# Weaving the blocks of w_down among those of w_up, with TensorE's order written out

## The chip, the cores and the metric

The kernel runs on one core of one Trainium2 chip. A core has TensorE (PE; its weight loads are listed apart as PEld), VectorE (DVE), ScalarE (ACT), GpSimd (POOL), a sync engine (SP) that issues plain loads and stores, and 16 DMA engines. The metric is the device time of one execution in microseconds, lower is better; the median of three runs is given.

## The reference

One decoder block on 512 tokens of width 1024, all in float32. Only the end of it bears on the change:

```python
merged = jax.nn.sigmoid(gate_a) * y_a + jax.nn.sigmoid(gate_b) * y_b
h = x + merged @ w_out[l]                     # 512x1024 @ 1024x1024
hn = rmsnorm(h, norm_mlp_g[l])
x = h + jnp.square(jax.nn.relu(hn @ w_up[l])) @ w_down[l]   # 1024 -> 4096 -> 1024
```

Ahead of it come a combined projection, a gated delta rule and a forgetting attention, which give y_a and y_b; with the gates they take the first 649 us, and the change touches them only where it is said below.

## The kernel before

**Precision.** Every float32 product is made of three float32r products: a matrix x is split into hi (x rounded to float32r, a cast on ScalarE) and lo (x minus hi, a subtraction on VectorE), and hi*hi + hi*lo + lo*hi are added up in PSUM. So each weight and each activation needs one cast and one subtraction before TensorE can use it.

**Seven products for eight.** w_o, w_up (w_u) and w_down (w_d) are cut in quarters, and a 2 x 2 block product is made of seven products P1 to P7 in Winograd's manner. w_up and w_down are worked through in four chunks c of 1024 of the 4096 hidden columns. So there are nine such block products: w_o, then for each chunk w_up and w_down. Each product has two units (`s_` 0 and 1), and a unit is one 128 x 1024 weight tile: 9 x 7 x 2 = 126 units. A unit of w_o or w_d is 12 matmuls of 512 columns, one of w_u 24 of 256.

*Weights* (`load`, L158): P1, P2 and P3 read a quarter fresh, on SP's queue; P5, P6, P4 and P7 add another quarter onto the tile of an earlier product (`FACTOR`, L144) by an accumulating DMA on GpSimd's queue, which must wait until VectorE has made the earlier product's low part. A ring of three raw tiles for each `s_` holds them. The look-ahead is `LA_RAW` = 3 and `LA_NEW` = 6 units for loads, `LA_SPLIT` = 2 for hi and lo (four buffers each; L203 casts, L204 subtracts).

*Activations* (`act_forms`, L927): P1, P2 and P4 take a quarter as it is, P5, P6, P3 and P7 a sum of quarters (L937 to L946), made on GpSimd for h and for the chunks, on VectorE for w_o. Then cast (L948) and low part (L949).

**Order.** `tokens_product` (L989) runs a whole block product of w_o or w_d in the order P1, P2, P5, P3, P6, P7, P4 and has VectorE add the PSUM banks into eight accumulator pages (L998). `mlp_up` (L1090) does the same for w_u, and evicts with a copy, or an addition, and relu and square on ScalarE (L1098 to L1110). One ends before the other is emitted: w_o, u0, d0, u1, d1, u2, d2, u3, d3. Between w_o and u0 lies the norm of h: squares on ScalarE (L1048), the inverse root (L1052 to L1054), scaling (L1061; the left half on VectorE, the right half on GpSimd), transposes on TensorE (L1067), and copies into the quarters `hq` (L1070). The blocks U, V and W of PSUM are chains of two banks; P1, P6, P7 and P4 go on in U, P5 and P3 in V.

What is emitted is not yet the order: a planner with a model of the engines orders each engine's instructions by priority (the place in the program) and readiness, gives out buffers from the free ones of a pool, and puts in the waits. The additions and evictions were given an earlier priority with `tc.high_priority(offset=AHEAD)`.

Of the kernel before, what the change touches and what calls it, by code (L numbers as in the profile page):

```python
# [16 lines left out]
P = 128  # L17
# [7 lines left out]
NACC = 12  # L25
NMM = 3
# [4 lines left out]
LA_NEW = 6  # L31
# [3 lines left out]
AHEAD = 150  # L35


def hybrid_block(tc, a, out):
# [24 lines left out]
    TAGS = {"junk": 2, "proj": 3}  # L63
# [83 lines left out]
    def product_units(w, c):  # L147
        return [(p, (w, c, s_)) for p in ORDER for s_ in range(NSUB)]

    seq += product_units("w_o", 0)  # L150
    for c in range(NC):
        seq += product_units("w_u", c) + product_units("w_d", c)
# [3 lines left out]
    fresh = [None, None]  # L156

    def load(n):  # L158
        nme, i = seq[n]
        if nme in FACTOR:  # L160
            w, c, s_ = i
            q, old = FACTOR[nme]
            if old is None:
                raw = fresh[s_].tile([P, D], F32, tag="raw", name=nm("draw"))
                nc.sync.dma_start(raw, a[w][c, q, s_])
            else:
                raw = factors[old, i]
                nc.gpsimd.dma_start(raw, a[w][c, q, s_], accum_op=ALU.add)
# [15 lines left out]
    def prefetch_new(n):  # L184

        for m in range(pos[0], min(len(seq), n)):
            if m not in raws and seq[m][0] in FACTOR and FACTOR[seq[m][0]][1] is None and fresh[0]:
                load(m)
# [725 lines left out]
    fresh[:] = [wraw, ctx.enter_context(tc.tile_pool(name="draw", bufs=3))]  # L914
# [12 lines left out]
    def act_forms(q, res, s_, order=("P1", "P2", "P5", "P6", "P3", "P7", "P4"), eng=None):  # L927


        eng = eng or vec  # L930
        for p in order:
# [3 lines left out]
            elif p == "P7":  # L935
                x = q[1, 0]
                eng.tensor_tensor(x, q[0, 0], x, op=ALU.subtract)  # L937
            elif p == "P5":
                x = s1 = accpage("s")
                eng.tensor_tensor(x, q[1, 0], q[1, 1], op=ALU.subtract)  # L940
            elif p == "P6":
                x = s2 = accpage("s")
                eng.tensor_tensor(x, s1, q[0, 0], op=ALU.subtract)
            else:
                x = accpage("s")
                eng.tensor_tensor(x, q[0, 1], s2, op=ALU.add)  # L946
            hi, lo = page(F32R, "shi"), page(F32R, "slo")
            act.copy(hi, x)  # L948
            vec.tensor_tensor(lo, x, hi[:, :].bitcast(F32), op=ALU.subtract)  # L949
            res[p, s_] = hi, lo  # L950
            yield

    def make(forms, gens, *products):
        for p in products:
            for s_ in range(NSUB):
                while (p, s_) not in forms:
                    next(gens[s_])
# [3 lines left out]
    mgens = [act_forms(merged[s_], mforms, s_) for s_ in range(NSUB)]  # L961
# [6 lines left out]
    for n in range(KT):  # L968
# [4 lines left out]
        for i in range(2):  # L973
            pool.tensor_tensor(of_half(merged[s_][i, j], f), of_half(sg, i), of_half(ma[n], i), op=ALU.add)
        for _ in range(2 if n >= 4 else 0):
            next(mgens[0], None)
# [12 lines left out]
    def tokens_product(w, c, gens, forms, done):  # L989


        chains, left = {}, {(0, 0): 2, (0, 1): 2, (1, 1): 2, (1, 0): 2 if w == "w_o" else 1}

        def add(i, l, ps, op):
            for t in range(2):
                acc = accs[2 * i + t][l]
                with tc.high_priority(offset=AHEAD):
                    vec.tensor_tensor(acc, acc, ps[t], op=op)  # L998
            left[i, l] -= 1
            if not left[i, l]:  # L1000
                done(i, l)

        for n, p in enumerate(ORDER):
            make(forms, gens, *ORDER[:n + 3])
            b, first = BANKS[p]
            if w == "w_o" and p == "P4":
                b, first = "X", True
            if first:
                chains[b] = [atps("down"), atps("down")]
            ps = chains[b]  # L1010
            for s_ in range(NSUB):
                whi, wlo = unit(p)
                shi, slo = forms[p, s_]
                for t in range(2):
                    for f in range(2):
                        wh, wl = whi[:, f * T:(f + 1) * T], wlo[:, f * T:(f + 1) * T]
                        k = slice(f * 256 + t * P, f * 256 + (t + 1) * P)
                        last = s_ == NSUB - 1 and f == 1
                        mm(ps[t], shi[:, k], wh, start=first and s_ == 0 and f == 0, stop=False, skip_group_check=True)  # L1019
                        mm(ps[t], slo[:, k], wh, start=False, stop=False, skip_group_check=True)  # L1020
                        mm(ps[t], shi[:, k], wl, start=False, stop=last, skip_group_check=True)  # L1021
                tick()
            if p in ("P1", "P2"):
                add(0, 0, ps, ALU.add)
            elif p == "P5":
                add(1, 1, ps, ALU.add)
            elif p == "P6":
                add(0, 1, ps, ALU.subtract)
            elif p == "P3":
                add(0, 1, ps, ALU.add)  # L1030
            elif p == "P7":
                if w == "w_o":
                    add(1, 0, ps, ALU.add)
                add(1, 1, ps, ALU.subtract)
            else:
                add(1, 0, ps, ALU.add)
# [4 lines left out]
    hgens = [act_forms(hq[s_], hforms, s_, eng=pool) for s_ in range(NSUB)]  # L1041
# [3 lines left out]
    def square_h(i, l):  # L1045
        for t in range(2):
            junk = page(s="junk")
            act.activation(junk, accs[2 * i + t][l], AF.Square, accum_out=ss_h[:, 2 * i + t, l:l + 1])  # L1048

    def normalise_h(i):  # L1050
        sl = slice(2 * i, 2 * i + 2)
        vec.tensor_tensor(rs_h[:, sl], ss_h[:, sl, 0], ss_h[:, sl, 1], op=ALU.add)  # L1052
        vec.tensor_scalar(rs_h[:, sl], rs_h[:, sl], 1.0 / D, EPS, op0=ALU.mult, op1=ALU.add)
        rsq(rs_h[:, sl], rs_h[:, sl])  # L1054
        for l in range(2):
            if i:
                yield
            hn = []
            for t in range(2):
                x = page(s="proj")  # L1060
                (pool if l else vec).tensor_scalar(x, accs[2 * i + t][l], rs_h[:, 2 * i + t:2 * i + t + 1], None, op0=ALU.mult)  # L1061
                hn.append(x)
            for j in range(2):
                pt = atps("hnT")
                for f in range(2):
                    for t in range(2):
                        nc.tensor.transpose(pt[:, f * 256 + t * P:f * 256 + (t + 1) * P], hn[t][:, cs(2 * j + f)], ident)  # L1067
                for f in range(2):
                    n = 4 * l + 2 * j + f
                    act.activation(of_half(hq[l][i, j], f), of_half(pt, f), AF.Copy, scale=mlp_g[:, n:n + 1])  # L1070
                if i == 0:
                    next(hgens[l])
        if i:
            make(hforms, hgens, "P5")
        yield
# [3 lines left out]
    def h_done(i, l):  # L1079
        square_h(i, l)  # L1080
        ready[i] -= 1
        if not ready[i]:
            ht.append(start(normalise_h(i)))
            if i == 0:
                finish(ht[0])

    ht = []
    tokens_product("w_o", 0, mgens, mforms, h_done)

    def mlp_up(c):  # L1090

        qs, chains, forms = quarters("act"), {}, {}
        gens = [act_forms(qs[s_], forms, s_, ("P1", "P2", "P4", "P5", "P6", "P3", "P7"), pool) for s_ in range(NSUB)]

        def evict(p, q, ps):

            if p == "P1":
                act.copy(q[0, 0], ps)  # L1098
            elif p == "P5":
                act.copy(q[1, 1], ps)  # L1100
            elif p == "P3":
                act.copy(q[0, 1], ps)
            elif p == "P4":
                act.activation(q[1, 0], ps, AF.Relu)
                act.activation(q[1, 0], q[1, 0], AF.Square)
            else:
                x, op = {"P2": (q[0, 0], ALU.add), "P6": (q[0, 1], ALU.subtract), "P7": (q[1, 1], ALU.subtract)}[p]
# [117 lines left out]
```

## Time and profile before

| | us |
|---|---|
| runs | 1056.85, 1056.90, 1054.27 (median 1056.85) |
| the profiled execution | 1054.39, its span 1052.7 |
| TensorE busy in the span | 1011.4 (96%) |
| VectorE, ScalarE, GpSimd busy | 688.7 (65%), 560.2 (53%), 285.1 (27%) |
| mean granted TensorE clock | 0.987 |
| DMA | 138.67 MB, mean 132 GB/s |

A matmul counts as busy up to its modelled end, which overlaps the next one, so TensorE's share says little about its pace; the starts of matmuls do. Low parts of weights (L204) carry 169.2 us of VectorE in this stage, of activations (L949) less. The time is to be read by stretches of the span, since the stages have different limits.

### The profile page before, as it was taken

How to read it: one execution, taken by the hardware profiler on the slowest of the kernel's cores; microseconds unless marked ns; L12 is line 12 of the kernel's file. 1: busy time of each engine (PE TensorE's matmuls, PEld its weight loads, DVE VectorE, ACT ScalarE, POOL GpSimd, SP SyncE). 2: the span in 40 equal slices, each digit the busy share in tenths (PEclk: the TensorE clock that was granted, in tenths of full speed). 3: DMA queues.
4: the chain of work that ended last, by engine and by line, in shares of the span. 5: the costliest groups of instructions: out<-in, count | busy, mean ns of one | idle time of the engine just before them, and what ended most of it. 6: DMA issues, size and time to landing. Idle time of an engine off the chain costs nothing.

```text
span 1052.7 us, 16282 instructions
## 1 busy us (share of the span) xinstructions
PE 1011.4 (96%) x6361; PEld 890.5 (85%) x6361; DVE 688.7 (65%) x1092; ACT 560.2 (53%) x855; POOL 285.1 (27%) x256
## 2 busy tenths in 40 slices
PE   9999999999999999999999999979899989989988
PEld 7788899998788999988888887779689869968966
DVE  6867777353678694445553238787885785686685
ACT  7674354355754545457633324485736735744751
POOL 1455120115343111021100034262421422251160
PEclk9999999999999999999999999999999999989999
DMA  6444323134233221325444336865589688777854
GB/s 216 142 127 138 92 85 95 60 101 140 71 120 109 72 91 52 92 100 148 133 160 160 100 109 155 197 140 137 124 176 199 156 168 186 182 144 174 189 114 116
DMA packets 58732, 138.67 MB, mean 132 GB/s; under 512 B 6208, under 2 KB 22816, under 8 KB 58656
## 3 DMA queue, kind: packets, MB, share of 16 engines
q1 hardware_dynamic: 48256, 99.88, 30.1%
q0 software_dynamic: 10400, 37.76, 20.7%
q8 instruction: 50, 0.82, 0.3%
q14 instruction: 26, 0.21, 0.1%
HBM read 129.18 MB, written 8.44 MB: 131 GB/s over the span
## 4 chain that ended last, share of the span: by engine, by line
PE 81%; DVE 10%; issue 4%; ACT 2%; DMA 1%; POOL 1%; SPq 0%; DVEq 0%; ACTq 0%; POOLq 0%
PE up L1130 14%; PE mm L222 9%; PE mm L223 9%; PE mm L226 9%; PE down L1021 4%; PE fx L810 4%; PE fx L813 4%; PE fx L811 4%; PE down L1019 4%; PE down L1020 4%; DVE lo L204 3%; DVE slo L949 2%; PE fo L793 2%; PE sc L768 2%; DVE acc L998 1%
## 5 line engine op out<-in xcount | busy, mean ns | idle before, releaser
L204 DVE TENSOR_TENSOR lo<-draw,hi 128x1024 fp32r<-128x1024 f32 x126 | 169.2, 1346 | 81.4 <-ACT hi L203 80.5
L203 ACT CAST hi<-draw 128x1024 fp32r<-128x1024 f32 x126 | 131.8, 1049 | 156.5 <-PE down L1020 76.9
L204 DVE TENSOR_TENSOR lo<-raw,hi 128x1024 fp32r<-128x1024 f32 (+1 forms) x90 | 111.8, 1248 | 87.6 <-PE mm L226 53.8
L203 ACT CAST hi<-raw 128x1024 fp32r<-128x1024 f32 (+1 forms) x90 | 91.9, 1029 | 110.4 <-PE mm L223 81.6
L222 PE MATMUL mm<-uhi,hi 128*128 128x512 f32 x344 | 136.1, 397 | 2.8 <-DVE conv L510 2.2
L223 PE MATMUL mm<-ulo,hi 128*128 128x512 f32 x344 | 136.6, 398 | 1.2 <-DVE ulo L237 1.2
L1021 PE MATMUL down<-lo,shi 128*128 128x512 f32 x280 | 111.4, 404 | 14.1 <-DVE lo L204 14.1
L1020 PE MATMUL down<-hi,slo 128*128 128x512 f32 x280 | 112.6, 403 | 6.4 <-DVE slo L949 6.4
L1019 PE MATMUL down<-hi,shi 128*128 128x512 f32 x280 | 109.8, 401 | 1.7 <-DVE sgb L972 0.9
L1130 PE MATMUL up<-slo,hi 128*128 128x256 f32 x448 | 92.6, 287 | 6.3 <-DVE slo L949 6.3
L810 PE MATMUL fx<-hi,uhi 128*128 128x256 f32 x384 | 97.9, 290 | 0.2 <-DVE conv L510 0.2
L811 PE MATMUL fx<-hi,ulo 128*128 128x256 f32 x384 | 96.0, 285 | 0.0
L1130 PE MATMUL up<-shi,hi 128*128 128x256 f32 x448 | 91.5, 285 | 1.7 <-ACT shi L948 1.1
L1130 PE MATMUL up<-shi,lo 128*128 128x256 f32 x448 | 90.3, 285 | 0.0
L226 PE MATMUL mm<-uhi,lo 128*128 128x512 f32 x344 | 89.2, 395 | 0.0
L222 PEld LDWEIGHTS mm<-uhi,hi 128*128 128x128 f32 x344 | 64.7, 188 | 17.7 <-issue 3.9
L223 PEld LDWEIGHTS mm<-ulo,hi 128*128 128x128 f32 x344 | 64.7, 188 | 15.4 <-DVE ulo L237 2.3
L1021 PEld LDWEIGHTS down<-lo,shi 128*128 128x128 f32 x280 | 54.7, 196 | 27.0 <-DVE lo L204 15.6
L1130 PEld LDWEIGHTS up<-slo,hi 128*128 128x128 f32 x448 | 71.0, 194 | 7.0 <-DVE slo L949 6.9
L226 PEld LDWEIGHTS mm<-uhi,lo 128*128 128x128 f32 x344 | 63.6, 188 | 13.3 <-issue 0.5
L810 PEld LDWEIGHTS fx<-hi,uhi 128*128 128x128 f32 x384 | 73.4, 191 | 1.2 <-issue 0.9
L811 PEld LDWEIGHTS fx<-hi,ulo 128*128 128x128 f32 x384 | 73.4, 191 | 0.5 <-issue 0.2
(309 smaller groups left out, 2112.7 us busy)
## 6 DMA issues: line engine op xcount, KB each, us to landing
draw<-w_u POOLq DMA_DIRECT2D x32, 512.0 KB, 6.9
draw<-w_d POOLq DMA_DIRECT2D x32, 512.0 KB, 5.6
raw<-w_gdn SPq DMA_DIRECT2D x24, 512.0 KB, 3.6
raw<-w_fox SPq DMA_DIRECT2D x24, 512.0 KB, 3.6
draw<-w_u SPq DMA_DIRECT2D x24, 512.0 KB, 4.2
draw<-w_d SPq DMA_DIRECT2D x24, 512.0 KB, 4.1
row<-rowd SPq DMA_DIRECT2D x24, 256.0 KB, 5.1
raw<-w_ga SPq DMA_DIRECT2D x8, 512.0 KB, 4.0
```

Of the source, the lines that this page charges most:

```text
L203: act.copy(hi[:, c], raw[:, c])
L204: vec.tensor_tensor(lo[:, c], raw[:, c], hi[:, c].bitcast(F32), op=ALU.subtract)
L222: mm(o, w, rhi(k), start=(k == 0), stop=False)
L223: mm(o, w, rlo(k), start=False, stop=False)
L226: mm(o, lo[:, k * cols:(k + 1) * cols], rhi(k), start=False, stop=(k == KT - 1))
L810: mm(o, uhi[k][:, cs(tb)], w, start=(k == 0), stop=False)
L811: mm(o, ulo[k][:, cs(tb)], w, start=False, stop=False)
L813: mm(o, uhi[k][:, cs(tb)], us[k // 4][1][:, (k % 4) * 256:(k % 4 + 1) * 256], start=False, stop=(k == KT - 1))
L1019: mm(ps[t], shi[:, k], wh, start=first and s_ == 0 and f == 0, stop=False, skip_group_check=True)
L1020: mm(ps[t], slo[:, k], wh, start=False, stop=False, skip_group_check=True)
L1021: mm(ps[t], shi[:, k], wl, start=False, stop=last, skip_group_check=True)
L1130: mm(o, wx[:, (2 * kb + f) * P:(2 * kb + f + 1) * P], of_half(hforms[p, j][part], kb % 2), start=first and f == 0 and part == 0 and wx is ...
```

## The change

- The 126 units get one written order, `MLP`. The units of w_d of a chunk stand among the last ones of w_u of the same chunk and the first ones of w_u of the next: for chunks after the first, w_u P5, w_d P4 of the chunk before, w_u P3, P6, P7, P4, w_d P1, P2, P5, w_u P1 of the next chunk, w_d P3, P6, w_u P2 of the next chunk, w_d P7. The last chunk has w_d P4 of the chunk before between its w_d P1 and P2, and its own P4 in banks of its own (as w_o).
- One loop over `MLP` takes the place of `tokens_product`'s and `mlp_up`'s loops. In each step it emits, in this order: transposes that are due, the cast of a weight, the evictions of the step before, the low part of the weight, loads, then small tasks on activations from a list `later`, up to two operations of VectorE in a step (three in w_o and in w_u's first chunk), and then the matmuls.
- TensorE's instructions of this part stay in program order (`tc.keep_in_program_order`). VectorE and ScalarE can be pinned in the same way from a given step on; with `PIN` = (400, 400, 0) and 126 steps they are not. The earlier priority of evictions goes.
- The sums of activations are made on VectorE, as is the whole scaling of h.
- P2's fresh tiles get a ring of their own with two tiles; the look-ahead is `LA_MLP` = 3 for hi and lo, `LA_RAW_MLP` = 5 and `LA_NEW` = 7 for loads; "proj" pages are four, not three. In the stage before, two half tasks (sum and cast, or low part) are taken after a product of w_pf where a whole one was taken twice.

```diff
     ORDER = ("P1", "P2", "P5", "P3", "P6", "P7", "P4")
+    MLP = [("w_o", 0, p, s_) for p, s_ in (("P1", 0), ("P2", 0), ("P1", 1), ("P2", 1))]
+    MLP += [(w, 0, p, s_) for w, ps in (("w_o", ORDER[2:]), ("w_u", ORDER[:2])) for p in ps for s_ in range(NSUB)]
+    for c in range(NC):
+        more = c + 1 < NC
+        MLP += [(w, c_, p, s_) for w, c_, p in (
+            ("w_u", c, "P5"), ("w_d", c - 1 if more else -1, "P4"), ("w_u", c, "P3"), ("w_u", c, "P6"), ("w_u", c, "P7"),
+            ("w_u", c, "P4"), ("w_d", c, "P1"), ("w_d", -1 if more else c - 1, "P4"), ("w_d", c, "P2"), ("w_d", c, "P5"),
+            ("w_u", c + 1, "P1"), ("w_d", c, "P3" if more else "P6"), ("w_d", c, "P6" if more else "P3"),
+            ("w_u", c + 1, "P2"), ("w_d", c, "P7")) for s_ in range(NSUB) if 0 <= c_ < NC]
+    MLP += [("w_d", NC - 1, "P4", s_) for s_ in range(NSUB)]
...
-                raw = fresh[s_].tile([P, D], F32, tag="raw", name=nm("draw"))
+                raw = fresh[2 if nme == "P2" else s_].tile([P, D], F32, tag="raw", name=nm("draw"))
...
+        def __getattr__(self, op):
+            f = getattr(self.eng, op)
+            return (lambda *args, **kw: tc.keep_in_program_order(f(*args, **kw))) if self.pinned[0] else f
...
+    def form_task(q, res, p, s_, steps):
+        if "a" in steps:
...
+                if p == "P5":
+                    pvec.tensor_tensor(x, q[1, 0], q[1, 1], op=ALU.subtract)
+                elif p == "P6":
+                    pvec.tensor_tensor(x, res["P5", s_, "x"], q[0, 0], op=ALU.subtract)
...
+        if "b" in steps:
+            hi = res[p, s_, "hi"]
+            lo = page(F32R, "slo")
+            pvec.tensor_tensor(lo, res[p, s_, "x"], hi[:, :].bitcast(F32), op=ALU.subtract)
...
-                with tc.high_priority(offset=AHEAD):
-                    vec.tensor_tensor(acc, acc, ps[t], op=op)
...
-                (pool if l else vec).tensor_scalar(x, accs[2 * i + t][l], rs_h[:, 2 * i + t:2 * i + t + 1], None, op0=ALU.mult)
+            pvec.tensor_scalar(x, accs[2 * i + t][l], rs_h[:, 2 * i + t:2 * i + t + 1], None, op0=ALU.mult)
...
+    for k, (w, c, p, s_) in enumerate(MLP):
+        for pin, first in zip(pins, PIN):
+            pin[0] = k >= first
+        used = 0
+        for f, *args in before:
+            f(*args)
+        del before[:]
+        n = pos[0]
+        pos[0] += 1
+        new = range(len(units), min(len(seq), n + 1 + LA_MLP))
+        for m in new:
+            hi, lo = whl.tile([P, D], F32R, tag="hi", name=nm("hi")), whl.tile([P, D], F32R, tag="lo", name=nm("lo"))
+            pact.copy(hi, raws[m][0])
+            units.append((hi, lo))
+        for f, *args in evicted:
+            f(*args)
+            used += f is add_task or (f is evict and args[0] in ("P2", "P6", "P7"))
+        for m in new:
+            hi, lo = units[m]
+            pvec.tensor_tensor(lo, raws[m][0], hi[:, :].bitcast(F32), op=ALU.subtract)
+        prefetch_raw(n + 1 + LA_RAW_MLP)
+        prefetch_new(n + 1 + LA_NEW)
+        res = {"w_o": mforms, "w_u": hforms}.get(w) or mlp[c][1]
+        needs = [(p, s_)] if w != "w_u" else [(p, j) for j in range(NSUB)]
+        while any(k not in res for k in needs) or later and used + cost(later[0]) <= (3 if w == "w_o" else 3 if w == "w_u" and c == 0 else PER_UNIT):
+            used += cost(later[0])
+            next_task()
+        ps, first = banks(w, c, p, s_)
+        if w == "w_u":
...
+            blocks_product(c, p, s_, [hforms[k] for k in needs], ps, first)
+            evicted = [(evict, p, qs[s_], ps[s_])]
...
+        else:
+            tokens_product(c, p, s_, res[p, s_], ps, first)
+            done = h_done if w == "w_o" else give if c == NC - 1 else lambda i, l: None
+            evicted = list(add_product(w, c, p, ps, done)) if s_ == NSUB - 1 else []
```

More of the change, by code (lines that the diff above doesn't have):

```diff
@@ L936, in act_forms, with forms_later, cost, next_task @@
                 x = q[1, 0]
[L937 to L943, printed above, removed]
+                pvec.tensor_tensor(x, q[0, 0], x, op=ALU.subtract)
             else:
                 x = accpage("s")
[L946 to L949, printed above, removed]
-            res[p, s_] = hi, lo
[L951 to L957, printed above, removed]
+                if p == "P5":
[3 more added lines that the diff above has]
+                else:
+                    pvec.tensor_tensor(x, q[0, 1], res["P6", s_, "x"], op=ALU.add)
+            hi = page(F32R, "shi")
+            pact.copy(hi, x)
+            res[p, s_, "x"], res[p, s_, "hi"] = x, hi
+        if "b" in steps:
+            hi = res[p, s_, "hi"]
+            lo = page(F32R, "slo")
+            pvec.tensor_tensor(lo, res[p, s_, "x"], hi[:, :].bitcast(F32), op=ALU.subtract)
+            res[p, s_] = hi, lo
+    def forms_later(qs, res, steps, parts=range(NSUB), front=False):
+        new = [(form_task, qs[s_], res, p, s_, st) for p, st in steps for s_ in parts]
+        later[:] = new + later if front else later + new
+    def cost(task):
+        f, *args = task
+        if f is count:
+            return 0
+        return 0 if f is form_task and args[2] in ("P1", "P2", "P4") and args[4] == "a" else 1
+    def next_task():
+        f, *args = later.pop(0)
+        f(*args)
     merged = quarters("m")
     mforms = {}
-    mgens = [act_forms(merged[s_], mforms, s_) for s_ in range(NSUB)]
     for n in range(KT):
@@ new lines, in hybrid_block, with apart, banks, tokens_product @@
+    banks_of, left = {}, {}
+    def apart(w, c):
+        return w == "w_o" or (w, c) == ("w_d", NC - 1)
+    def banks(w, c, p, s_):
+        b, first = ("X", True) if apart(w, c) and p == "P4" else BANKS[p]
+        if first and s_ == 0:
+            banks_of[w, c, b] = [atps("mlp"), atps("mlp")]
+        return banks_of[w, c, b], first
+    def tokens_product(c, p, s_, form, ps, first):
+        whi, wlo = units[pos[0] - 1]
+        shi, slo = form
+        for t in range(2):
+            for f in range(2):
+                wh, wl = whi[:, f * T:(f + 1) * T], wlo[:, f * T:(f + 1) * T]
+                k = slice(f * 256 + t * P, f * 256 + (t + 1) * P)
+                last = s_ == NSUB - 1 and f == 1
+                ppe.matmul(ps[t], shi[:, k], wh, start=first and s_ == 0 and f == 0, stop=False, skip_group_check=True)
+                ppe.matmul(ps[t], slo[:, k], wh, start=False, stop=False, skip_group_check=True)
+                ppe.matmul(ps[t], shi[:, k], wl, start=False, stop=last, skip_group_check=True)
@@ new lines, in add_task, with count, add_product @@
+    def add_task(acc, ps, op):
+        pvec.tensor_tensor(acc, acc, ps, op=op)
+    def count(w, c, i, l, done):
+        n = left[w, c, i, l] = left.get((w, c, i, l), 0) + 1
+        if n == (1 if not apart(w, c) and (i, l) == (1, 0) else 2):
+            done(i, l)
+    def add_product(w, c, p, ps, done):
+        add, sub = ALU.add, ALU.subtract
+        for i, l, op in {"P1": [(0, 0, add)], "P2": [(0, 0, add)], "P5": [(1, 1, add)], "P3": [(0, 1, add)],
+                         "P6": [(0, 1, sub)], "P7": [(1, 1, sub)] + ([(1, 0, add)] if apart(w, c) else []),
+                         "P4": [(1, 0, add)]}[p]:
+            for t in range(2):
+                yield add_task, accs[2 * i + t][l], ps[t], op
+            yield count, w, c, i, l, done
@@ L1039, in hybrid_block, with h_done @@
     hq = quarters("hq")
     hforms = {}
-    hgens = [act_forms(hq[s_], hforms, s_, eng=pool) for s_ in range(NSUB)]
     rs_h = const([P, NCH], "rs_h")
     ss_h = const([P, NCH, 2], "ss_h")
-    def square_h(i, l):
+    before = []
+    ready = [2, 2]
+    def h_done(i, l):
         for t in range(2):
             junk = page(s="junk")
[L1048 to L1075, printed above, removed]
@@ new lines, in h_done, with rms_h, scale_h @@
+            later[:0] = [(rms_h, i), (scale_h, i, 0), (scale_h, i, 1)]
+    def rms_h(i):
+        sl = slice(2 * i, 2 * i + 2)
+        pvec.tensor_tensor(rs_h[:, sl], ss_h[:, sl, 0], ss_h[:, sl, 1], op=ALU.add)
+        pvec.tensor_scalar(rs_h[:, sl], rs_h[:, sl], 1.0 / D, EPS, op0=ALU.mult, op1=ALU.add)
+        rsq(rs_h[:, sl], rs_h[:, sl])
+    def scale_h(i, l):
+        hn = []
+        for t in range(2):
+            x = page(s="proj")
+            pvec.tensor_scalar(x, accs[2 * i + t][l], rs_h[:, 2 * i + t:2 * i + t + 1], None, op0=ALU.mult)
+            hn.append(x)
+        before.append((turn_h, i, l, hn))
@@ L1131, in mlp_up, with blocks_product @@
+    def blocks_product(c, p, s_, forms, ps, first):
+        whi, wlo = units[pos[0] - 1]
+        for j in range(2):
+            for f in range(2):
+                o = of_half(ps[s_], f)
+                for part, wx in ((0, whi), (1, whi), (0, wlo)):
+                    for kb in (2 * j, 2 * j + 1):
+                        ppe.matmul(o, wx[:, (2 * kb + f) * P:(2 * kb + f + 1) * P], of_half(forms[j][part], kb % 2),
                                    start=first and f == 0 and part == 0 and wx is whi and kb == 0,
```

177 lines of the change are left out of this document (68 added, 109 removed).

## The prediction

> **What bounds the kernel now.** I read the page's head first, then busy time by stretch, then two undisturbed stretches, TensorE's waits, and the instructions around its longest stop.
>
> ```profile
> span 1052.7 us, 16282 instructions
> ```
>
> ```profile
> 0.00:648.70 648.70, 640.94 (x4145) 561.16 (x4145) 389.04 (x786) 334.66 (x537) 154.95 (x139) 1.00 0.38 115
> 648.70:1048.60 399.90, 370.43 (x2216) 329.33 (x2216) 299.08 (x307) 225.56 (x318) 130.19 (x118) 0.97 0.73 159
> 1048.60:1052.70 4.10, 0.00 (x0) 0.00 (x0) 0.60 (x1) 0.00 (x0) 0.00 (x0) 1.00 0.17 64
> ```
>
> The columns are the stretch, its length, busy time of PE, PEld, DVE, ACT, POOL, granted clock, DMA share and GB/s. Before 648.70 us TensorE is busy 641 of 649 us. From there to 1048.60 us run the output projection (w_o), w_up and w_down: the stage that the change rewrites, and the one with gaps. 4.10 us of write-out follow.
>
> What the stage would take without a stop comes from two stretches where TensorE runs undisturbed, in the chain of waits and in the timeline:
>
> ```profile
> 791.30 35.75 PE up L1130 x298
> 1046.05 0.39 PE L1021 MATMUL down<-lo,shi 128*128 128x512 f32 x1
> 1048.09 0.39 PE L1021 MATMUL down<-lo,shi 128*128 128x512 f32 x1
> ```
>
> A 256-column matmul issues every 35.75 / 298 = 0.120 us. The last ten 512-column ones start over 2.04 us, so 0.2267 us each. The stage has 70 units of w_o and w_down with 12 of the wide ones (840) and 56 of w_up with 24 of the narrow ones (1344), and 32 transposes, at 1.25 us for ten (row below). That is 190.4 + 161.3 + 4.0 = 355.7 us. The stage takes 399.9, so **44 us are lost**. By stretch:
>
> ```profile
> 648.70:689.00 40.30, 39.41 (x178) 32.52 (x179) 32.31 (x43) 23.00 (x37) 14.05 (x13) 1.00 0.67 149
> 689.00:785.20 96.20, 82.91 (x510) 74.00 (x509) 82.78 (x78) 58.85 (x92) 38.21 (x33) 0.95 0.68 151
> 785.20:870.80 85.60, 80.58 (x506) 72.68 (x505) 61.35 (x63) 48.61 (x64) 25.95 (x24) 0.98 0.80 173
> 870.80:957.90 87.10, 82.04 (x506) 73.75 (x505) 61.38 (x63) 48.60 (x64) 26.01 (x25) 0.96 0.78 170
> 957.90:1048.60 90.70, 85.49 (x524) 76.38 (x522) 61.26 (x64) 46.50 (x62) 25.97 (x24) 0.96 0.69 148
> ```
>
> Multiplying the counts by the two rates, some 20 us go up to 785 us (w_o and the first chunk), and some 7 to 8 in each of the three other chunks. What TensorE waits for:
>
> ```profile
> PE down L1021 <- DVE lo L204: 14.1, 3, 4.7
> PE down L1020 <- DVE slo L949: 6.4, 5, 2.9
> PE up L1130 <- DVE slo L949: 6.3, 2, 5.7
> ```
>
> VectorE, by far, yet it is busy only 299 of the 400 us. It is late in bursts: after a chunk's last w_up block, the sums and low parts that w_down needs all fall due at once, with no matmul to cover them. And the bursts are stretched:
>
> ```profile
> 705.01 6.15 DVE L949 TENSOR_TENSOR slo<-s,shi 128x512 fp32r<-128x512 f32 x1
> 705.39 1.58 POOL L937 TENSOR_TENSOR hq<-hq,hq 128x512 f32<-128x512 f32 x1
> 709.05 1.56 POOL L937 TENSOR_TENSOR hq<-hq,hq 128x512 f32<-128x512 f32 x1
> 711.22 0.80 PE L1130 MATMUL up<-slo,hi 128*128 128x256 f32 x2 [5.67 <-DVE slo L949]
> 711.22 7.26 PE up L1130 x42
> 711.20:713.50 2.30, 2.28 (x10) 0.50 0.01 2
> ```
>
> One low part took 6.15 us while GpSimd ran four sums back to back, TensorE stood 5.67 us for it, and then 42 narrow matmuls took 7.26 us instead of 5.04, at a granted clock of 0.50 first. So a long stop costs about 2.2 us more than itself.
>
> **The change, part by part.** *Sums to VectorE.* The grouped rows:
>
> ```profile
> L204 DVE TENSOR_TENSOR lo<-draw,hi 128x1024 fp32r<-128x1024 f32 x126 | 169.2, 1346 | 81.4 <-ACT hi L203 80.5
> L949 DVE TENSOR_TENSOR slo<-s,shi 128x512 fp32r<-128x512 f32 x36 | 45.2, 1282 | 0.0
> L949 DVE TENSOR_TENSOR slo<-hq,shi 128x512 fp32r<-128x512 f32 x8 | 5.4, 687 | 0.3 <-ACT shi L948 0.3
> L203 ACT CAST hi<-draw 128x1024 fp32r<-128x1024 f32 x126 | 131.8, 1049 | 156.5 <-PE down L1020 76.9
> L948 ACT CAST shi<-hq 128x512 fp32r<-128x512 f32 x8 | 5.0, 621 | 0.1
> L998 DVE TENSOR_TENSOR acc<-acc,down 128x512 f32<-128x512 f32 x72 | 48.0, 681 | 8.6 <-PE down L1021 8.5
> 768.29 0.68 DVE L998 TENSOR_TENSOR acc<-acc,down 128x512 f32<-128x512 f32 x1
> 768.89 0.68 DVE L949 TENSOR_TENSOR slo<-s,shi 128x512 fp32r<-128x512 f32 x1
> 770.09 1.21 DVE L204 TENSOR_TENSOR lo<-draw,hi 128x1024 fp32r<-128x1024 f32 x1
> 771.22 0.68 DVE L949 TENSOR_TENSOR slo<-s,shi 128x512 fp32r<-128x512 f32 x1
> ```
>
> 40 sums (4 products, 2 halves, the normalised h and four chunks) leave GpSimd at about 1.6 us (rows at 705.39 and 709.05) and arrive on VectorE at 0.69 (the nearest row of two such operands): +27.6 us. The collisions go: 36 x (1.282 - 0.687) = 21 us, and 126 x (1.346 - 1.21) = 17. VectorE ends about 10 us lighter. In a queue the small operations start 0.60 us apart (768.29, 768.89) and a low part of a weight takes 1.13 (770.09 to 771.22).
>
> *The weave.* In a later chunk VectorE has 28 weight low parts and 42 small operations (14 low parts, 8 sums, 14 adds, 6 evictions): 28 x 1.13 + 42 x 0.60 = 57 us for 78.4 us of matmuls. Beside one weight part at most two small operations fall on a unit (1.13 + 2 x 0.60 = 2.3 us against 2.72), because the new loop stops handing out tasks at two. The sums after the last w_up block now have w_down's first two products (and in the last chunk the previous chunk's P4) in front of them: 10.9 or 16.3 us of matmuls for a sum, a cast and a low part of under 0.7 us each, twice. I take 4 us left of today's 23 in these chunks (one each and one at the end, where nothing is left to weave); bounds 0 and 15. The stop where a bank is added up before the next block continues it is also covered, by the blocks put between.
>
> *The beginning* keeps a part of its loss, since there is no w_down yet to weave.
>
> ```profile
> 682.59 1.25 PE L1067 MATMUL hnT<-ident,proj 128*128 128x128 f32 x10
> 688.91 0.39 PE L1021 MATMUL down<-lo,shi 128*128 128x512 f32 x1
> 694.46 1.32 DVE L1061 TENSOR_SCALAR proj<-acc,rs_h 128x512 f32<-128x512 f32 x2 [0.62 <-POOL rs_h L295]
> L1070 ACT ACTIVATE hq<-hnT,c_norm_mlp_g 128x256 f32<-128x256 f32 x16 | 6.6, 473 | 0.3 <-PE hnT L1067 0.3
> ```
>
> From w_o's last matmul to the first scaling of h go 5.55 us; four scalings (all on VectorE now) 2.64; together 8.2. The pinned order puts the transposes after two units of w_up, 5.8 us: a stop of 2.4, with every later matmul queued behind it. The same chain for the first half of the tokens has two units of w_o, 5.4 us, in front of it: 2.8. Behind each set of 16 transposes come 8 copies (3.8 us), a sum, a cast and a low part (2.0), with two weight casts of 1.05 between them on ScalarE, against 2.0 us of transposes and two units: 1 each. VectorE's demand over these 28 units (29 low parts, 13 sums, 16 adds, 6 evictions, 8 scalings) is 28 x 1.13 + 72 x 0.60 = 75 us of 82: 1 more. That makes **8 us** of today's 20; bounds 3 (most of the chain hidden) and 20.
>
> The two stops of 2.4 us bring up the clock:
>
> ```profile
> 758.12 0.50 PE L1020 MATMUL down<-hi,slo 128*128 128x512 f32 x1 [2.89 <-DVE slo L949]
> 758.00:760.70 2.70, 2.58 (x11) 1.00 0.49 64
> 763.50:766.00 2.50, 2.42 (x6) 0.50 0.75 93
> ```
>
> After 2.89 us of standing the clock stayed at 1.00; after the next stop, close behind it, it was 0.50. I count no drop, and two (4.4 us) in the range. The Trainium skill, "TensorE: Matmul & The Clock Gate", section "HAM oscillation — how this bites in real kernels", warns of idle gaps above about 3.4 us, which speaks against an order in which TensorE stands rather than takes other work. By that rule two stops of under 3 us add nothing to the sum; the last row here shows a drop behind a shorter one, so the trace agrees only in part.
>
> *Loads.* The third ring of raw tiles and the longer look-ahead cost no time; accumulating loads still lie at least four units behind the product that they add to, as now. On SP's and GpSimd's queues they are issued in the new order; a load that waits for its tile holds those behind it, as today, and GpSimd has no sums before them any more. TensorE ran at full pace at these loads:
>
> ```profile
> 791.30:827.00 35.70, 35.70 (x300) 35.70 (x299) 23.30 (x25) 25.47 (x36) 6.47 (x8) 1.00 0.87 190
> draw<-w_u POOLq DMA_DIRECT2D x32, 512.0 KB, 6.9
> ```
>
> The first 649 us change only by the planner's reshuffling (one more "proj" buffer, half tasks): 0, within 2 us.
>
> **Sum.** 355.7 + 8 + 4 = 367.7 us for the stage: 32.2 less. The profiled execution took 1054.39 us, so 1022.2; the median of the runs shown, 1056.85, lies 2.5 above it. I forecast 1024. Its own range: from 3 + 0 (1015) to 13 + 8 (1033).
>
> **Rivals.** *The beginning stays bound* by VectorE and the normalisation chain, and the planner's order on VectorE and ScalarE, no longer raised for evictions, keeps half of the later loss: 20 + 11 = 31 us lost of 44, a gain of 13: 1044. For it: 75 of 82 us demand and no spare work. Against: the collisions are gone, which made the longest stop.
>
> *The loads become the bound.* 126 x 0.524 = 66 MB at the 173 GB/s of the second chunk are 382 us, 26 above the floor; 18 gained: 1039. Against: 190 GB/s at 0.87 in the row above.
>
> *Slower:* accumulating loads turn late. Each tile is read by VectorE, added to by DMA, and split again; where that lies four units apart (three places in a chunk) there are 11.2 us for the landing plus a cast and a low part (1.05 + 1.21), so it holds to 8.9 us. Each us beyond costs TensorE, now pinned and unable to go round it, up to 3 x 4 = 12 us in all. From 11.6 us of landing (8.9 + 32 / 12) it eats the gain. At 14 us: 61 us against 32, so 1085. For it: median 6.9 at 0.87 share is close. Against: two units of look-ahead in split weights lie between.
>
> **How the numbers follow.** The forecast 0.66, the beginning 0.14, the loads 0.07, slower 0.08; 0.03 that it is the same (TensorE's stops only move), 0.02 below 1015. A difference of 0.3%, 3 us, is what a measurement can tell from none. Faster 0.89, same 0.03, slower 0.08. The range for 8 in 10 takes in the forecast's own and the two partial cases: 1015 to 1045.
>
> **What would show it.** Right: no GpSimd tensor operation after the start of w_o, low parts of sums at 0.69 us, weight low parts near 1.22; three later chunks of 79 to 80 us; TensorE's remaining waits at the transposes and the first P5 of w_up, 2 to 3 us each. Wrong: waits of TensorE on low parts inside later chunks, low parts above 1.3 us without GpSimd sums, a DMA landing above 8 us, or a granted clock of 0.50 past the first chunk.

## The result, and the profile after

The changed kernel takes **1024.21 us** (median of four runs, 1021.73 to 1026.12) against 1055.56 for the kernel before (four runs, 1052.53 to 1056.90): a ratio of 0.9706, 95% interval 0.9674 to 0.9737. The profiled execution took 1024.1 us.

The head of its page, two of its rows of groups, and the two rows of accumulating loads (the last number is the median from issue to landing, in us):

```profile
span 1022.4 us, 16241 instructions
PE 1003.3 (98%) x6361; PEld 887.9 (87%) x6361; DVE 674.4 (66%) x1138; ACT 561.5 (55%) x855; POOL 219.8 (21%) x212
...
L1172 DVE TENSOR_TENSOR lo<-draw,hi 128x1024 fp32r<-128x1024 f32 x124 | 151.2, 1222 | 54.8 <-ACT hi L1165 54.7
...
draw<-w_u POOLq DMA_DIRECT2D x32, 512.0 KB, 5.8
draw<-w_d POOLq DMA_DIRECT2D x32, 512.0 KB, 6.5
```

```profile
L978 DVE TENSOR_TENSOR slo<-s,shi 128x512 fp32r<-128x512 f32 x36 | 24.4, 712 | 0.0
```

Low parts of weights take 1.222 us each where they took 1.346, low parts of sums 0.712 where they took 1.282. Landings did not get shorter: 5.8 against 6.9 us for w_u, but 6.5 against 5.6 for w_d. Over the whole stage the accumulating loads of w_o, w_up and w_down land after 6.1 us in the median and 9.5 at the longest, where it was 6.2 and 9.1.

Busy time by stretch, with the columns of the prediction (length, busy PE, PEld, DVE, ACT, POOL, granted clock, DMA share, GB/s). First what lies ahead of the stage and the stage itself, then the stage cut where TensorE's stops begin and end:

```profile
0.00:651.70 651.70, 643.17 (x4145) 563.42 (x4146) 387.68 (x784) 333.46 (x535) 155.40 (x139) 0.99 0.37 116
651.70:1018.40 366.70, 360.09 (x2216) 324.48 (x2216) 286.10 (x355) 228.01 (x320) 64.39 (x74) 0.99 0.77 171
```

```profile
651.60:706.30 54.70, 49.82 (x250) 42.21 (x251) 43.77 (x62) 33.38 (x59) 12.60 (x14) 0.97 0.76 165
706.30:950.40 244.10, 244.10 (x1608) 225.15 (x1607) 193.53 (x232) 159.62 (x216) 44.24 (x52) 1.00 0.83 183
950.40:1018.40 68.00, 66.18 (x363) 57.13 (x361) 48.90 (x62) 35.00 (x46) 7.59 (x9) 0.97 0.59 132
```

The stage takes 366.7 us where it took 399.9, so 33.2 of the gain lie there. 2.9 of them are given back ahead of it, where TensorE's first matmul of w_o starts at 651.71 and not 648.74. The chain of waits says the same of the middle stretch more sharply, and shows what is left at both ends:

```profile
687.22 1.75 PE hnT L946 x16
...
701.08 1.25 DVE lo L1172
...
702.87 3.46 PE hnT L946 x16
706.33 244.14 PE mlp L946 x1606
...
996.79 6.76 DMA draw<-w_d
...
1003.65 1.05 ACT hi L1165
1004.73 1.24 DVE lo L1172
...
1006.01 12.33 PE mlp L946 x46
```

For 244 us TensorE's own pace is the chain: 480 wide and 1127 narrow matmuls, at the two rates of the prediction 244.0 us. Nothing at all is lost from the third unit of w_up into the last chunk. At the end the chain leaves TensorE for a landing of w_down. All that TensorE waits for from w_o to the end (us in total, times, longest):

```profile
PE hnT L946 <- DVE proj L1100: 2.7, 1, 2.7
PE mlp L946 <- DVE acc L1055: 1.9, 1, 1.9
PE mlp L946 <- ACT hi L1165: 1.2, 1, 1.2
PE mlp L946 <- DVE sgb L1008: 0.9, 1, 0.9
PE mlp L946 <- DVE lo L1172: 0.5, 1, 0.5
```

Against the 355.7 us that the matmuls need, the stage loses 11.0 us: 6.8 up to 706.3 (its 168 wide and 48 narrow matmuls and 32 transposes are 47.9 us of 54.6), none in the middle, 4.2 at the end (192 wide and 169 narrow are 63.8 of 68.0).

### The profile page after: what moved, and what is told of

It reads as the page before. It is cut to its first block, busy times and chain, and to the rows that moved or that the text cites. A ratio compares the mean times of both kernels' runs of the same rounds, so it can differ in the third digit from the quotient of the medians.

```text
span 1022.4 us, 16241 instructions
## 1 busy us (share of the span) xinstructions
PE 1003.3 (98%) x6361; PEld 887.9 (87%) x6361; DVE 674.4 (66%) x1138; ACT 561.5 (55%) x855; POOL 219.8 (21%) x212
## 4 chain that ended last, share of the span: by engine, by line
PE 85%; DVE 4%; issue 4%; DMA 4%; POOL 1%; ACT 1%; SPq 0%; POOLq 0%; DVEq 0%; ACTq 0%
PE mlp L946 29%; PE mm L233 9%; PE mm L234 9%; PE mm L237 9%; PE fx L824 5%; PE fx L821 5%; PE fx L822 5%; DMA draw<-w_d 2%; PE fo L804 2%; PE sc L779 2%; DMA row<-rowd 1%; PE pT L795 1%; PE v L668 1%; DVE conv L521 1%; PE o L687 1%
## 5 line engine op out<-in xcount | busy, mean ns | idle before, releaser
L1172 DVE TENSOR_TENSOR lo<-draw,hi 128x1024 fp32r<-128x1024 f32 x124 | 151.2, 1222 | 54.8 <-ACT hi L1165 54.7
L946 PE MATMUL mlp<-hi,shi 128*128 128x512 f32 x280 | 110.3, 394 | 4.2 <-DVE acc L1055 1.9
L946 PE MATMUL mlp<-lo,shi 128*128 128x512 f32 x280 | 109.7, 392 | 0.5 <-DVE lo L1172 0.5
L946 PE MATMUL mlp<-hi,slo 128*128 128x512 f32 x280 | 109.7, 392 | 0.0
L946 PE MATMUL mlp<-slo,hi 128*128 128x256 f32 x448 | 90.3, 283 | 0.0
L946 PE MATMUL mlp<-shi,lo 128*128 128x256 f32 x448 | 90.3, 283 | 0.0
L946 PE MATMUL mlp<-shi,hi 128*128 128x256 f32 x448 | 90.3, 283 | 0.0
L946 PEld LDWEIGHTS mlp<-shi,hi 128*128 128x128 f32 x448 | 70.6, 192 | 0.9
L946 PEld LDWEIGHTS mlp<-shi,lo 128*128 128x128 f32 x448 | 69.9, 192 | 0.0
```

What stands on the lines that cost most here:

```text
L946: return (lambda *args, **kw: tc.keep_in_program_order(f(*args, **kw))) if self.pinned[0] else f
L1172: pvec.tensor_tensor(lo, raws[m][0], hi[:, :].bitcast(F32), op=ALU.subtract)
```

## The experiments

The time of the kernel before, on the same chips, lay at 1055.1 to 1056.8 us; ratios are against it, with their 95% interval.

### E1: the kernel before, with nothing but its sums moved

```diff
-    hgens = [act_forms(hq[s_], hforms, s_, eng=pool) for s_ in range(NSUB)]
+    hgens = [act_forms(hq[s_], hforms, s_) for s_ in range(NSUB)]
...
-        gens = [act_forms(qs[s_], forms, s_, ("P1", "P2", "P4", "P5", "P6", "P3", "P7"), pool) for s_ in range(NSUB)]
+        gens = [act_forms(qs[s_], forms, s_, ("P1", "P2", "P4", "P5", "P6", "P3", "P7")) for s_ in range(NSUB)]
```

> The kernel before, with one part of the change alone: the sums of activations of h and of the four chunks are made on VectorE, not on GpSimd; order, priorities and scaling stay. Theory A (cover): TensorE stands because sums and low parts fall due at once with no matmuls in front of them; then this alone gains 6 to 10 us of the 31 (1046 to 1050), and the waits at the turn from w_up to w_down stay, shorter. Theory B (collisions): TensorE stands because GpSimd's sums hold VectorE up; then this alone gains 20 us or more (1036 or less). In both, low parts of sums take 0.69 us, not 1.28, and weight low parts 1.22.

1034.65 us, ratio 0.9794 (0.9773 to 0.9815): 22 us faster, two thirds of the whole change's gain from two lines, as theory B had it (20 or more). Its low parts, and some of the sums that VectorE now makes:

```profile
L204 DVE TENSOR_TENSOR lo<-draw,hi 128x1024 fp32r<-128x1024 f32 x126 | 153.9, 1224 | 71.8 <-ACT hi L203 71.8
L949 DVE TENSOR_TENSOR slo<-s,shi 128x512 fp32r<-128x512 f32 x36 | 24.6, 698 | 0.0
L943 DVE TENSOR_TENSOR s<-s,act 128x512 f32<-128x512 f32 x8 | 5.5, 684 | 0.0
```

and what TensorE still waits for in this stage:

```profile
PE down L1019 <- DVE acc L998: 7.9, 5, 1.8
PE down L1021 <- DVE lo L204: 4.9, 4, 1.4
PE up L1130 <- ACT shi L948: 1.8, 2, 1.0
PE up L1130 <- DVE slo L949: 1.5, 2, 1.1
```

Both durations fall to what the changed kernel shows, in the old order, so the fall comes from taking the sums off GpSimd and not from the order. The longest stop, 5.7 us before, is 1.8. The largest part of the stops that are left are additions of a bank that the next product continues: the order's share.

### E2 and E3: the changed kernel without the move, and without the weave

E2 gives the sums of h and of the chunks back to GpSimd, in the woven order:

```diff
     def form_task(q, res, p, s_, steps):
+        eng = pvec if res is mforms else pool
...
-                pvec.tensor_tensor(x, q[0, 0], x, op=ALU.subtract)
+                eng.tensor_tensor(x, q[0, 0], x, op=ALU.subtract)
...
```

> The changed kernel with the sums of activations of h and the chunks back on GpSimd, the weave and the pinned order kept. Theory A (cover): the stretched low parts hide under the woven matmuls, so at most 6 us are lost against the changed kernel (1024 to 1030). Theory B (collisions): 15 us or more are lost (1039 or more). In both, low parts of sums go back to some 1.3 us and single ones to 3 us or more.

1032.1 us, ratio 0.9774 (0.9735 to 0.9813): 7 to 8 us slower than the changed kernel. That lies between the two theories, nearer to A (at most 6) than to B (15 or more).

```profile
L1173 DVE TENSOR_TENSOR lo<-draw,hi 128x1024 fp32r<-128x1024 f32 x124 | 162.9, 1317 | 67.7 <-ACT hi L1166 67.6
...
L979 DVE TENSOR_TENSOR slo<-s,shi 128x512 fp32r<-128x512 f32 x36 | 33.8, 967 | 4.1 <-ACT shi L974 4.1
...
L970 POOL TENSOR_TENSOR s<-s,act 128x512 f32<-128x512 f32 x8 | 15.9, 2011 | 0.0
```

The low parts are slow again, 1.317 and 0.967 us, though less than the 1.346 and 1.282 before: the new loop hands out at most two small operations in a step, which fits that sums and low parts now meet less often; no run tests that reason. The woven order hides more than half of what the collisions cost (8 us are left of the 22 in E1), not all.

E3 keeps everything of the change but the order of the units, which is that of the kernel before:

```diff
-    for c in range(NC):
-        more = c + 1 < NC
-        MLP += [(w, c_, p, s_) for w, c_, p in (
...
+    MLP = [u for u in MLP if u[0] == "w_o"]
+    MLP += [(w, c, p, s_) for c in range(NC) for w in ("w_u", "w_d") for p in ORDER for s_ in range(NSUB)]
```

> The changed kernel with its loop, its pinned TensorE and its sums on VectorE, but the units in the order of before: all of w_up of a chunk, then all of w_down. Theory A (cover): most of the gain goes: each of the four turns from w_up to w_down stops TensorE for 4 us or more, 1044 to 1054. Theory B (collisions): 1030 or less.

1040.83 us, ratio 0.9852 (0.9830 to 0.9874): some 16 slower than the changed kernel, which again lies between the two theories (1044 to 1054 by A, 1030 or less by B). It is 6 slower than E1, which makes the sums on the same engine and has the same order of units but leaves TensorE's instructions to the planner.

```profile
PE mlp L940 <- DVE acc L1049: 14.3, 5, 3.4
PE hnT L940 <- DVE proj L1094: 2.7, 1, 2.7
```

No low part is waited for; five additions of banks are, 14.3 us (1.95 of them in w_o, the rest in the four chunks), where E1 had 7.9 in five. In this loop the additions of a product are emitted in the step after it and have lost their earlier priority, and where nothing lies between two products in one bank, TensorE stands for them. So the new loop is worth its gain only together with the weave. (E3 changes more than one thing against E1, so how much of the 6 us is the pin, the missing priority or another part of the loop isn't settled.)

With E1 to E3 the two parts can be set side by side:

| | old order | woven order and its loop |
|---|---|---|
| sums on GpSimd | 1056 | 1032.1 (E2) |
| sums on VectorE | 1034.65 (E1) | 1024.2 |

Either part alone brings 22 to 25 us, both 31: they remove largely the same stops.

### E4: the pin alone taken away

```diff
-PIN = (400, 400, 0)
+PIN = (400, 400, 400)
```

> The changed kernel with TensorE not pinned, all else the same. If the written order needs the pin, the planner takes matmuls out of it and 8 us or more are lost (1032 or more), with TensorE's order near w_o and the first chunk different from the written one. If the weave alone does it, the time stays within 4 us of the changed kernel (1020 to 1028). By the rival in which pinned TensorE stands where it could do other work, it gets faster by 3 us or more (1021 or less), since the stop at the second transposes (2.7 us and a slow clock behind it) would be filled.

1024.55 us (1019.92 to 1025.88), ratio 0.969 (0.9659 to 0.972): no difference from the changed kernel. The planner's order, with the woven program, is as good as the written one. The two traces show differences that largely cancel. The second transposes no longer stop TensorE (ten of them at 702.34, six at 705.11), as the rival had it, but in the last chunk TensorE stands longer for a weight's cast than in the changed kernel (1.23 us there, 1.17 and 3.27 here):

```profile
702.34 1.25 PE L1109 MATMUL hnT<-ident,proj 128*128 128x128 f32 x10
1007.54 0.80 PE L1050 MATMUL mlp<-hi,shi 128*128 128x512 f32 x1 [3.27 <-ACT hi L1165]
```

### E5: the end of the last chunk, with a longer distance

The stop at the end of the chain (a cast at 1003.65 and a low part at 1004.73, for which TensorE waits 1.23 and 0.53 us) is that of a unit whose load was issued late. About four units are left then (46 matmuls), P7 and P4, so the unit is the first of P7. In the last chunk the order is w_d P5, P6, P3, P7, so P6 is added onto P5's tile, and P7 onto P3's, only **two** units later. E5 sets P5, P3, P6, P2, P7, P4 there, which puts every accumulating load at least four units behind. P3 then needs a bank pair of its own, at the price of two more additions; the sums of that chunk are made in the usual order again.

```diff
-    MLP += [("w_d", NC - 1, "P4", s_) for s_ in range(NSUB)]
+    MLP = MLP[:-10] + [("w_d", NC - 1, p, s_) for p in ("P5", "P3", "P6", "P2", "P7", "P4") for s_ in range(NSUB)]
...
-        b, first = ("X", True) if apart(w, c) and p == "P4" else BANKS[p]
+        b, first = ("X", True) if apart(w, c) and p == "P4" else ("Y", True) if (w, c, p) == ("w_d", NC - 1, "P3") else BANKS[p]
...
```

> The changed kernel with the end of the last chunk in another order: w_d P1, P4 of the chunk before, P5, P3, P6, P2, P7, P4, so that each accumulating load lies at least four units behind the product that it adds to (P6 lies two units behind P5, and P7 two behind P3, in the changed kernel); P3 gets a pair of banks of its own, which costs two more additions. Theory: the stop near 1004 us and the clock of 0.56 behind it come from those two distances of two units (5.4 us for a landing of 5.8 us, a cast and a low part), so both vanish and 3 to 4 us are gained (1020 to 1021). Rival: the loads are late because the DMA engines are full there; then the stop stays, whatever the order, and the time stays within 2 us of the changed kernel.

**1018.89 us** (1018.49 to 1021.26), ratio 0.9669 (0.9655 to 0.9683) against the changed kernel's 0.9706 (0.9674 to 0.9737): 4 to 5 us better by these, though the two intervals overlap a little. E6 below, which keeps the changed kernel's stop at the end, has 0.9716 (0.9695 to 0.9737), clear of E5. In the profiled executions the stage takes 363.1 us (649.66 to 1012.76) against 366.7, so 3.6 us are gained where the edit acts, as the theory had it; the other 2 us lie ahead of w_o, where nothing was changed. TensorE now runs from the third unit of w_up to the end without a stop:

```profile
704.55 308.20 PE mlp L946 x1968
1012.76 0.69 DVE acc L1055
```

The stop is gone, and with it the low clock that followed it in the changed kernel (PE, granted clock, DMA share, GB/s of four us there):

```profile
1006.00:1010.00 4.00, 3.99 (x11) 0.57 0.18 66
```

The rival of full DMA engines, by which the stop would stay, falls. So the distance was the cause: E5 also gives P3 its own banks and another order of sums, but the chain of the stop held neither, only the load, its cast and its low part.

### E6 and E7: the chain of the norm first

TensorE's longest stop, 2.7 us at the second 16 transposes, waits for the scaling of h, and low parts of weights stand in that chain. E6 gives the inverse root and the scaling an earlier priority; E7 is E5 and E6 together.

```diff
     def rms_h(i):
+        with tc.high_priority(offset=150):
+            rms_h_(i)
+
+    def scale_h(i, l):
+        with tc.high_priority(offset=150):
+            scale_h_(i, l)
...
```

> The changed kernel with an earlier priority (150 places) for the small operations between the squares of h and the transposes (sum of squares, mean, root, scaling), so that they no longer stand behind weight low parts in VectorE's order. Theory: the stop of 2.7 us at the second transposes and the half clock behind it (16 transposes in 3.46 us, not 1.75) come from three low parts put before them (1.2 us each); then the stop shrinks to under 1 us and 3 to 4 us are gained (1020 to 1021). Rival: the chain itself is the bound (additions, squares, root, scaling one after the other), then less than 1 us is gained.

> The two edits of the runs on the end of the last chunk and on the order of h's small operations together. If their stops are separate, the gains add up: 6 to 8 us, 1016 to 1018. If one only moves the other, 4 us or less.

E6: 1025.15 us, ratio 0.9716 (0.9695 to 0.9737); E7: 1019.15, ratio 0.9665 (0.9652 to 0.9678). E6 doesn't differ from the changed kernel, nor E7 from E5 (1018.89), and the stop is 2.67 us still. ScalarE, VectorE and GpSimd in E6 ahead of it:

```profile
695.59 0.23 ACT L1085 ACTIVATION_READ_ACCUMULATOR junk<-acc 128x1 f32 x1
695.79 1.22 DVE L1180 TENSOR_TENSOR lo<-draw,hi 128x1024 fp32r<-128x1024 f32 x1
696.93 0.15 DVE L1100 TENSOR_TENSOR rs_h<-ss_h 128x2 f32<-128x2 f32 x1
697.00 1.22 DVE L1180 TENSOR_TENSOR lo<-draw,hi 128x1024 fp32r<-128x1024 f32 x1
698.13 0.17 DVE L1101 TENSOR_SCALAR rs_h<-rs_h 128x2 f32<-128x2 f32 x1
699.08 1.03 POOL L306 TENSOR_TENSOR rs_h<-rs_h,expo 128x2 f32<-128x2 f32 x1
699.44 1.25 DVE L1180 TENSOR_TENSOR lo<-draw,hi 128x1024 fp32r<-128x1024 f32 x1 [1.14 <-ACT hi L1173]
700.61 1.66 DVE L1108 TENSOR_SCALAR proj<-acc,rs_h 128x512 f32<-128x512 f32 x4
```

The priority moved nothing: VectorE's operations stand in the same order here as in the changed kernel's trace, the same three low parts among them. So E6 and E7 test neither theory by their times. The rows themselves speak for the low parts. The last square is ready at 695.82 (695.59 and 0.23), and its sum starts at 696.93, behind a low part: 1.1 us. The mean, which needs that sum (696.93 and 0.15, 697.08), starts at 698.13, behind the next one: 1.05. The root is ready at 700.11 (699.08 and 1.03), and the scaling starts at 700.61, behind the third: 0.5. Together that is about 2.65 us, as long as the stop itself. This is an estimate from one trace; no run has the low parts moved out of the way, so what the norm's chain would cost without them is open.

### E8 to E10: the bank in w_o, and the clock

E8 is E5 with a bank pair of its own for w_o's P3 too, E9 is E5 with 20 transposes of the identity, whose result nobody reads, in front of the second set of transposes, and E10 is both.

```diff
-        b, first = ("X", True) if apart(w, c) and p == "P4" else ("Y", True) if (w, c, p) == ("w_d", NC - 1, "P3") else BANKS[p]
+        b, first = ("X", True) if apart(w, c) and p == "P4" else ("Y", True) if apart(w, c) and p == "P3" else BANKS[p]
...
```

```diff
             pt = atps("hnT")
+            for z in range(20 if (i, l, j) == (1, 0, 0) else 0):
+                ppe.transpose(pt[:, (z % 4) * P:(z % 4 + 1) * P], ident, ident)
```

> The kernel with the longer distance in the last chunk, and in w_o too P3 gets a bank pair of its own (P5 is then added to accumulator (0,1) as well: two more additions on VectorE). Theory C: the 1.95 us stop between w_o's P5 and P3 is the wait for the addition that empties their common bank, so with a bank of its own that stop is gone and the time falls by about 1.9 us (1017 against 1018.9). Theory D: VectorE's queue is what is late there, and the same wait comes back at the next product that needs something of VectorE in w_o or at the transposes; with two more additions (1.2 us) the time stays at 1018.5 to 1020.

> The kernel with the longer distance in the last chunk, with 20 transposes of the identity, whose result nobody reads, put on TensorE ahead of the second set of 16 transposes of h, where it stands 2.67 us. Theory E: standing 2.67 us is what halves the granted clock, so with the filler (20 x 0.12 = 2.4 us) the stop is under 0.5 us, the clock stays at 1.00 there, the 16 transposes take 1.9 us instead of 3.2 to 3.7, and the time falls by 1.5 to 2.5 us (1016.5 to 1017.5). Theory F: the clock falls there for another reason than the standing (the kind of instruction, the small tiles); then the 16 transposes still take over 3 us and the time stays within 1 us of 1018.9.

> Both edits at once: by C and E together 1014.5 to 1016; by C alone 1017; by E alone 1017; by neither 1019 to 1020.

| | us | ratio to the kernel before |
|---|---|---|
| E5 | 1018.89 | 0.9669 (0.9655 to 0.9683) |
| E8 | 1019.93 | 0.9661 (0.9642 to 0.9681) |
| E9 | 1019.24 | 0.9660 (0.9644 to 0.9676) |
| E10 | 1017.89 | 0.9646 (0.9629 to 0.9664) |

The intervals overlap: none of the three can be told from E5 by its time. E8 lies where theory D had it (1018.5 to 1020), E9 where F had it (within 1 us of 1018.9), and E10 between the forecasts for one theory (1017) and for neither (1019 to 1020). The traces say more. TensorE's stops in E8:

```profile
678.98 0.47 PE L946 MATMUL mlp<-hi,shi 128*128 128x512 f32 x1 [1.35 <-DVE acc L1055]
686.32 3.00 PE L946 MATMUL hnT<-ident,proj 128*128 128x128 f32 x16 [1.66 <-DVE proj L1100]
```

The stop between P5 and P3 is gone, as both theories had it, and 1.35 us come back at a later bank and 1.66 at the first transposes: VectorE's queue is late there, and the wait moves (theory D). In E9, the second transposes:

```profile
699.05 2.35 PE L946 MATMUL hnT<-ident 128*128 128x128 f32 x20
701.78 2.25 PE L946 MATMUL hnT<-ident,proj 128*128 128x128 f32 x16 [0.39 <-DVE proj L1100]
```

beside the same in the changed kernel, where TensorE stood, and its first set, where it did not:

```profile
687.06 1.91 PE L946 MATMUL hnT<-ident,proj 128*128 128x128 f32 x16
...
702.87 3.46 PE L946 MATMUL hnT<-ident,proj 128*128 128x128 f32 x16 [2.67 <-DVE proj L1100]
```

With the filler 16 transposes take 2.25 us, not 3.46. The granted clock there, the changed kernel first and then E9 (PE, granted clock, DMA share, GB/s):

```profile
704.00:706.00 2.00, 2.00 (x12) 0.53 1.06 182
```

```profile
702.00:704.00 2.00, 1.94 (x18) 1.00 1.00 180
```

All seven profiled executions in which TensorE stands some 2.7 us there (the changed kernel, E2, E3 and E5 to E8) show a clock of 0.50 to 0.53 behind it; E9 and E10, with the filler, show 1.00. So it was the standing that brought the clock down (theory E's mechanism). But what the filler saves there is not in the median, which theory E had at 1016.5 to 1017.5. In the profiled execution it was lost at another stop: the one of 1.93 us in w_o was followed by a lower clock here, and by none in E5. The first row is E9 behind that stop, the second E5 (busy TensorE, granted clock, DMA share, GB/s):

```profile
665.00:670.00 5.00, 3.07 (x11) 0.84 0.84 140
```

```profile
665.00:670.00 5.00, 3.06 (x14) 1.00 0.75 121
```

## Why the prediction was right, and where a step failed

**The forecast held:** 1024.0 against 1024.21, and by its own sum a stage of 367.7 us against 366.7. That the time agrees to 0.2 us is luck: the sum gives 1024.7 (1022.2 and 2.5), and the first part of the profiled execution took 2.9 us more than assumed. The stage, within 1 us, is the better test, and there too two terms came out near their size from other stops than those named. Of its terms:

- **The floor of 355.7 us** and the two rates held; the middle stretch runs at them to 0.1 us.
- **Sums to VectorE.** Right in mechanism and size: 1.222 and 0.712 us against 1.21 and 0.687 assumed. VectorE's busy time in the stage fell by 13 us (299.08 to 286.10), where "about 10" was forecast. E1 shows that GpSimd is the cause. What the prediction did not say, and E1 and E2 show, is how the 31 us split: by themselves the sums bring 22, and the weave and its loop 9 to 10 on top; taken the other way round, the weave and its loop bring 24 to 25, and the sums 7 to 8 on top.
- **The weave.** "4 us left (one each and one at the end)": the total was right, its place wrong. The three chunks lost nothing, not one each, and the last 68 us lost 4.2. There the step that failed is the one on loads: "accumulating loads still lie at least four units behind the product that they add to". In the last chunk they lie two behind, as the list in the diff shows (P6 straight behind P5). Two units of 2.72 us cannot cover a landing of 6.5 us plus a cast and a low part (1.05 and 1.24). The units split ahead still covered P6, the first of the two; TensorE stopped for P7. E5 gives the distance back, and the stage gains 3.6 us. It is also the one place where the rival of late accumulating loads came about; elsewhere single landings of up to 9.5 us, above its 8.9, stopped nothing.
- **"The stop where a bank is added up ... is also covered, by the blocks put between"**: right in the chunks, where no such stop is left, and E3 shows that without those blocks it is some 12.4 us there (14.3 less the 1.95 in w_o). Wrong in w_o, where nothing is put between P5 and P3: 1.95 us.
- **The beginning**, 8 us forecast, 6.8 measured, from other parts than those named. The second transposes stopped 2.67 us (2.4 forecast); by the estimate under E6, low parts of weights in the norm's chain, which the prediction doesn't name, make up most of that. The first, forecast at 2.8, didn't stop, and neither did TensorE at the first P5 of w_up. In their place came the bank stop in w_o (1.95) and the term set to nothing: "I count no drop" in the clock. A stop of 2.67 us did halve it, for some 1.2 to 1.6 us of time: the same 16 transposes took 3.46 us behind it, and at full clock 1.91 for the set without a stop and 2.25 behind the stop of 0.39 in E9.
- **The first 649 us** were to change by 0, within 2; the profiled execution has 2.9 more. A difference of that size need not come from the change: w_o's first matmul began at 648.07 to 652.60 us in the profiled executions of the experiments, 651.65 in E1, whose first part is that of the kernel before, and 648.44 in E6, whose first part is that of the changed kernel.
- **The pin** was taken for a risk, since TensorE can't go round a late unit. E4 shows no effect on the time; without the pin the stop at the second transposes goes and the one in the last chunk grows.
- **The rivals.** A beginning that stays bound was to lose 20 us and lost 6.8. Loads as the bound, at 173 GB/s, didn't come about either: the middle stretch ran without a stop at 183.

Of the signs to look for, the 0.71 and 1.22 us came out right, and GpSimd is left without any sum of quarters and any scaling. The length of a chunk can't be read, since the chunks now overlap, but the middle stretch has no stop. Of the signs for "wrong", two showed in the last chunk: a wait on a low part (0.5 us, behind 1.2 for its cast) and a low granted clock (0.57), and they pointed at the step on loads. The third, landings above 8 us, showed too (9.5), but the kernel before had them as well (9.1), so that sign could tell nothing.

## What to carry to other kernels

Before reordering work around an engine that is late in bursts, measure the durations of its operations with the neighbour that it collides with and without: two lines (E1) brought two thirds of what a rewritten loop did. In a written order, go through the distance between each load and the instruction that frees its tile for **every** place in the list, the last round above all, where nothing is left to fill it. Two parts of a change that remove the same stops don't add up: price each alone and both together. And when an experiment shows no effect, see in the trace whether its edit moved what it was to move (E6), and whether two effects cancel (E4).

## What the runs showed of the hardware

- **The clock falls after stops well under 3 us.** Sixteen transposes took 1.91 us with no stop ahead in the changed kernel, 3.46 behind one of 2.67 us, and 3.00 behind one of 1.66 (E8). Behind the stop of 1.93 to 1.95 us in w_o the clock stayed at 1.00 in three profiled executions (the changed kernel, E5, E7) and fell to 0.60 or less over 2 us in four (E2, E3, E6, E9). So a drop can follow a stop of less than 2 us, and whether it does differs between executions. The Trainium skill, "TensorE: Matmul & The Clock Gate", section "HAM oscillation — how this bites in real kernels", puts the danger at idle gaps above about 3.4 us. By these rows it begins lower. The same page of the Trainium skill, section "What's actually happening", says that the activity window runs freely and does not start anew with the kernel. That would fit the difference between executions; no run here shows the window itself.
- **GpSimd's sums slow VectorE's two-operand operations** by 0.12 us in 1.22 and 0.58 in 0.70 on the mean in the old order (before against E1), by 0.10 and 0.26 in the woven one (E2 against the changed kernel). GpSimd also takes longer for the same sum (2.01 us for the sums from s and act in E2, 0.684 on VectorE in E1). There are as many sums and low parts in both orders, so the price of a collision depends on how the operations meet, not only on how many there are.
- **The best kernel of these is the changed one with the longer distance at its end** (E5, 1018.89 us); the fillers and extra banks of E8 to E10 could not be told from it.
